# A decoder block on one core: the output projection as seven block products, its right operands built between the steps of the last attention-output products

## The chip, the core and the metric

The kernel runs on one core of one Trainium2 chip. The metric is the device time of one execution in microseconds (us). The core has engines that run side by side: TensorE (PE, matmuls into the accumulators of PSUM), VectorE (DVE), ScalarE (ACT), GpSimd (POOL) and SyncE (SP), whose queue issues nearly all DMA transfers of the part that is changed. Each engine takes its instructions in the order in which they were put into its queue, and waits on semaphores for the others.

## The reference, cut to what matters

One layer with SEQ = 2048 positions and D_MODEL = 1024 channels. Two branches (a gated recurrence and an attention in three window and dilation patterns) give `hr` and `o`; what the change touches is the end:

```python
y_rnn = (hr * silu(z_rnn)) @ w_out_rnn
y_attn = (o * silu(z_attn)) @ w_out_attn
merged = sigmoid(g_r + bg_r) * y_rnn + sigmoid(g_a + bg_a) * y_attn
x = x + gate[:, None, :] * (merged @ w_o)
return rms_norm(x, g_final)
```

## The kernel before, in words

All matmuls take float32 operands in two halves, a high and a low one, and do three matmuls (`mm3`, L149: high x high, high x low, low x high). The high half is a copy on ACT, the low half a subtraction on POOL (`lo_pool`) or DVE (`lo_dve`).

The input projection computes its large products by a scheme with seven block products in place of eight (`strassen`, L272). A left operand (two blocks of 128 columns, in two halves of the inner dimension) is turned into seven tiles `S` by sums on DVE (`left_operands`, L236), each split by `split_s`; the right operands B11, T2, T3, T1, B21, T4, B22 are held in SBUF. A product is 4 x 3 matmuls of 128x512; the products accumulate into four PSUM tiles X, Z, W, V, with three sums u1, u2, u3 on ACT and DVE between. In the first half of the sequence the `S` are built and also stored to memory, in the second they are loaded (`stored_operands`).

Then comes the attention, 16 heads of six units, laid out by hand in slots (`tc.manual_schedule`, L1381): in each slot run the scores of one unit, the softmax, the transposes and sums of earlier ones, and in between a number of steps of a generator, `steps` (L1277), the fill. It does the products with `w_out_rnn` (four jobs, one for each quarter n of the sequence) and with `w_out_attn` (two jobs, n = 0 and 1). A job has eight tiles m, a tile eight steps k, a step one `mm3`. Within a tile, SP gets in this order: a half tile of weights w at k = 1 (four buffers, so three halves ahead), the gates of the tile at k = 3 (`load_g`: gaT and mrT into two tiles of the ring "fg" of four buffers), the next half of w at k = 5, and at k = 7 the store of the tile before (meT). The eviction of the tile before stands at k = 1 on DVE. Near the end of a job the next job's left side y is loaded and split. `FILL` (L34) sets how many steps a slot gets: 3.6 in the first half of the heads, 3.2 in the second. Slots run from -5 to 105; the first rate holds for 60 of them, the second for 51. What is left of the fill runs behind the last slot.

After that the automatic scheduler takes over. Buffers for `w_o` are opened where the attention had its own; eight pieces of 128 rows of `w_o` are loaded, multiplied by the residual gate and split into `oh` and `ol` (L1429 to L1434). `output(n)` (L1436) does one quarter of the sequence: for each of four row blocks r it loads x and the merged columns from meT, splits these, does two halves of 512 columns of 8 x 3 matmuls, adds x, takes the mean square, scales, and stores. Between the four calls stand the attention-output products of n = 2 and 3 (`attn_product`, L1461), by `product` (L1254), which loads y, w and the gates in the scheduler's order with the same ring "fg" (`done_attn`, L1240).

Of the kernel before, what the change touches and what calls it, by code (L numbers as in the profile page):

```python
# [20 lines left out]
P = 128  # L21
S = 2048
# [11 lines left out]
FILL = (3.6, 3.2)  # L34
# [50 lines left out]
def decoder_block(ctx, tc, x, c, positions, g_norm, w_mod, b_mod, w_in, b_gate, conv_w, conv_b,  # L85
# [100 lines left out]
    def split_s(src):  # L186
        t = T(wq, [P, 2, KH, P], F32R, "S", bufs=7)
        last_hi[0] = nc.scalar.activation(t[:, 0], src, AF.Copy).ins  # L188
        lo_pool(t[:, 1], src, t[:, 0])
        return t  # L190
# [45 lines left out]
    def left_operands(pieces):  # L236

        a11, a12, a21, a22 = blocks(pieces)
        yield split_s(a11)
        s1 = T(wq, [P, KH, P], F32, "s1", bufs=1)  # L240
        s2 = T(wq, [P, KH, P], F32, "s2", bufs=1)
        nc.vector.tensor_tensor(s1[:], a21, a22, ALU.add)
        nc.vector.tensor_tensor(s2[:], s1[:], a11, ALU.subtract)
        yield split_s(s2[:])
        nc.vector.tensor_tensor(a21, a11, a21, ALU.subtract)
        yield split_s(a21)
        yield split_s(s1[:])
        yield split_s(a12)
        yield split_s(a22)
        nc.vector.tensor_tensor(s2[:], a12, s2[:], ALU.subtract)  # L250
        yield split_s(s2[:])

    def first_operands(x, pieces):

        for i, t in enumerate(left_operands(pieces)):
# [16 lines left out]
    def strassen(up, f, key, pieces, done):  # L272

        x = pair_id.setdefault(key, len(pair_id))
        ops = stored_operands(x) if f else first_operands(x, pieces)

        def prod(ps, b, first, last):
# [5 lines left out]
            n_prod[0] += 1  # L283
            run_late(n_prod[0])

        X = T(pj, [P, CH], F32, "pj")
        prod(X, "B11", True, False)
        Z = T(pj, [P, CH], F32, "pj")
# [6 lines left out]
        W = T(pj, [P, CH], F32, "pj")  # L295
# [4 lines left out]
        V = T(pj, [P, CH], F32, "pj")  # L300
# [933 lines left out]
    def done_rnn(ps, rows, cn):  # L1234
        g = T(fl, [P, CH], F32, "fg", bufs=4)
        nc.sync.dma_start(g[:], grT[rows, cn])
        nc.vector.tensor_tensor(g[:], ps[:], g[:], ALU.mult)
        nc.sync.dma_start(mrT[rows, cn], g[:])

    def done_attn(ps, rows, cn):  # L1240
        g = T(fl, [P, CH], F32, "fg", bufs=4)
        nc.sync.dma_start(g[:], gaT[rows, cn])
        r = T(fl, [P, CH], F32, "fg", bufs=4)
        nc.sync.dma_start(r[:], mrT[rows, cn])
        nc.vector.tensor_tensor(g[:], ps[:], g[:], ALU.mult)
        nc.vector.tensor_tensor(g[:], g[:], r[:], ALU.add)
        nc.sync.dma_start(meT[rows, cn], g[:])

# [4 lines left out]

    def product(w, ys, n, done):  # L1254

        cn = slice(n * CH, (n + 1) * CH)
        yt = []
        for k in range(KT):
# [7 lines left out]
        for m in range(KT):  # L1266
            rows = slice(m * P, (m + 1) * P)
            ps = T(pj, [P, CH], F32, "pj")
            for k in range(KT):
                if k % KH == 0:  # L1270
                    wt = load_wd(w, m, k // KH)
# [229 lines left out]
```

## Time and profile before

| What | us |
|---|---|
| median of 3 runs | 2367.67 |
| lowest and highest | 2366.49, 2369.38 |
| the profiled execution's own time | 2364.77 |
| its span in the profile | 2363.0 |

The profile is one execution. The page gives busy time, share of the span and instruction count of each engine, and then the span in 40 slices of 59 us with a digit for the busy tenths. PEld is the weight load, which overlaps PE. PEclk and "clock" are the granted clock of TensorE as a part of full speed. A timeline row has start, duration, engine, line, operation, output<-input, shape and count, and in brackets the idle time before it with the releaser. A row by windows has the stretch, its length, then busy time with the count for each engine, the clock, the mean busy share of the 16 DMA engines and GB/s. A row of the waits has who waited for whom, the total, the number of times and the longest. A row of a group has count, busy time, mean ns of one, and the idle time before it with its releasers. Lines L147, L161 and L164 are helpers. The tile names tell the groups apart: `pj` are projection products, `pq` the output projection, `fg` the gates, `w` the weights of the attention-output and recurrence-output products.

### The profile page before, as it was taken

To read this page: it belongs to the slowest core of one execution; us is meant where nothing else is said; L and a number is where in the kernel's file an instruction comes from. 1 tells how busy PE (TensorE), PEld (TensorE's weight loads), DVE (VectorE), ACT (ScalarE), POOL (GpSimd) and SP (SyncE) were. 2 spreads that over 40 slices of the span, in tenths; PEclk is the share of its full clock that TensorE was granted. 3 is DMA by queue.
4 is the path that set the end of the run, shared out by engine and by line. 5 is a ranking of instruction groups with operands and counts; after the bars stand their busy time and mean duration, and the time that the engine had idled before them with its cause. 6 is when DMAs were issued, how large, how long until landed. Compare 5 with 4: busy or idle time off the path is not lost.

```text
span 2363.0 us, 34030 instructions
## 1 busy us (share of the span) xinstructions
PE 2232.6 (94%) x11397; PEld 1877.8 (79%) x11397; DVE 1340.2 (57%) x2423; ACT 1170.4 (50%) x2332; POOL 1003.8 (42%) x765
## 2 busy tenths in 40 slices
PE   5999999999999989999999998799999999989998
PEld 5897777777777888888888877688888898978887
DVE  6847666666575653544444462266666777645433
ACT  3436656666642434655444410366667878622111
POOL 2566656665555553433121110355445656443000
PEclk9999999999999999999999999899999999999999
DMA  7266777777788639999776776888999889797652
GB/s 266 82 207 235 267 240 259 255 248 249 251 272 251 205 120 322 326 346 314 247 243 231 222 264 212 259 262 255 300 299 273 263 248 287 217 337 275 225 178 97
DMA packets 420902, 585.44 MB, mean 248 GB/s; under 512 B 72446, under 2 KB 278518, under 8 KB 419704
## 3 DMA queue, kind: packets, MB, share of 16 engines
q1 hardware_dynamic: 383288, 463.72, 62.9%
q10 hardware_dynamic: 37440, 119.55, 13.3%
q8 instruction: 90, 1.47, 0.2%
q14 instruction: 84, 0.69, 0.1%
HBM read 367.14 MB, written 216.01 MB: 247 GB/s over the span
## 4 chain that ended last, share of the span: by engine, by line
PE 61%; DMA 12%; DVE 11%; ACT 5%; issue 5%; POOL 3%; SPq 2%; ACTq 1%; DVEq 0%; POOLq 0%
PE pj L147 43%; PE pq L147 7%; PE o L147 3%; PE sc L147 3%; PE pg L147 2%; DMA wraw<-in_w_in_dram 2%; POOL S L161 1%; PE pT L1082 1%; DMA w<-wD 1%; DVE acc L487 1%; DMA wD<-s 1%; ACT S L188 1%; DMA kraw<-qT 1%; PE pT L1095 1%; DMA qT<-t 1%
## 5 line engine op out<-in xcount | busy, mean ns | idle before, releaser
L147 PE MATMUL pj<-T,S 128*128 128x512 f32 x4704 | 1119.5, 398 | 33.7 <-DVE ev L340 15.7
L147 PEld LDWEIGHTS pj<-T,S 128*128 128x128 f32 x4704 | 887.8, 189 | 254.0 <-DVE ev L340 21.1
L147 PE MATMUL pj<-yh,w 128*128 128x512 f32 x1024 | 371.7, 408 | 11.7 <-ACT yh L155 10.4
L161 POOL TENSOR_TENSOR S<-wraw,S 128x512 fp32r<-128x512 f32 x168 | 240.7, 1444 | 175.8 <-ACT S L188 100.5
L147 PEld LDWEIGHTS pj<-yh,w 128*128 128x128 f32 x1024 | 195.6, 191 | 50.3 <-ACT yh L155 12.5
L147 PE MATMUL pj<-yl,w 128*128 128x512 f32 x512 | 204.0, 399 | 2.3 <-POOL yl L161 1.4
L998 ACT ACTIVATE pp<-pp,st 128x256 f32<-128x256 f32 (+3 forms) x256 | 133.8, 524 | 89.5 <-DVE st L997 88.7
L147 PE MATMUL pj<-S,T 128*128 128x256 f32 x1152 | 161.9, 297 | 10.3 <-POOL S L161 7.0
L147 PEld LDWEIGHTS pj<-S,T 128*128 128x128 f32 x1152 | 151.9, 202 | 12.3 <-POOL S L161 8.0
L161 POOL TENSOR_TENSOR S<-s,S 128x512 fp32r<-128x512 f32 x84 | 114.7, 1366 | 89.7 <-ACT S L188 43.7
L164 DVE TENSOR_TENSOR ptl<-pT,pth 128x384 fp32r<-128x384 f32 (+1 forms) x160 | 97.8, 628 | 60.8 <-ACT pth L155 58.6
L1062 ACT ACTIVATE pp<-pp,M 128x256 f32<-128x256 f32 (+3 forms) x256 | 118.0, 523 | 12.7 <-DVE M L1186 12.7
L642 DVE SCALAR_TENSOR_TENSOR xc<-xr,par,xc 128x512 f32<-128x512 f32 x96 | 87.0, 907 | 61.2 <-ACT xc L636 58.1
L997 DVE CUSTOM_DVE_ANT_0 pp<-sc,msk 128x256 f32<-128x256 f32 (+3 forms) x256 | 105.2, 449 | 24.6 <-PE sc L147 21.4
L294 DVE TENSOR_TENSOR u<-pj,u 128x512 f32<-128x512 f32 x56 | 38.4, 686 | 140.8 <-PE pj L147 91.1
L147 PEld LDWEIGHTS pj<-yl,w 128*128 128x128 f32 x512 | 98.1, 192 | 18.5 <-POOL yl L161 2.6
L161 POOL TENSOR_TENSOR kq<-kraw,kq 128x512 fp32r<-128x512 f32 (+1 forms) x64 | 100.4, 1578 | 19.4 <-ACT kq L155 13.9
L161 POOL TENSOR_TENSOR vh<-vraw,vh 128x256 fp32r<-128x256 f32 (+1 forms) x64 | 66.4, 1037 | 94.8 <-ACT vh L155 83.1
L161 POOL TENSOR_TENSOR wh<-vraw,wh 128x640 fp32r<-128x640 f32 (+1 forms) x32 | 48.4, 1513 | 135.2 <-ACT wh L155 74.7
L147 PE MATMUL pq<-oh,mh 128*128 128x512 f32 x256 | 98.0, 394 | 7.9 <-ACT mh L155 7.9
L147 PE MATMUL pq<-ol,mh 128*128 128x512 f32 x256 | 100.8, 394 | 0.3 <-POOL ol L161 0.3
L147 PE MATMUL pq<-oh,ml 128*128 128x512 f32 x256 | 99.6, 390 | 0.0
(290 smaller groups left out, 3886.2 us busy)
## 6 DMA issues: line engine op xcount, KB each, us to landing
sD<-S ACTq DMA_DIRECT2D x196, 512.0 KB, 3.1
S<-sD SPq DMA_DIRECT2D x196, 512.0 KB, 5.4
w<-wD SPq DMA_DIRECT2D x128, 512.0 KB, 6.2
wraw<-in_w_in_dram SPq DMA_DIRECT2D x136, 256.0 KB, 3.3
wD<-s ACTq DMA_DIRECT2D x64, 256.0 KB, 4.1
T<-in_w_mod_dram SPq DMA_DIRECT2D x8, 1024.0 KB
vN<-ev SPq DMA_DIRECT2D x64, 128.0 KB, 2.5
zaT<-ev SPq DMA_DIRECT2D x32, 256.0 KB, 2.8
```

The lines of the kernel that those rows point to most:

```text
L147: last_mm[0] = nc.tensor.matmul(o, lhsT=l, rhs=r, start=st, stop=sp, **kw).ins
L161: nc.gpsimd.tensor_tensor(o, i, h.bitcast(F32), ALU.subtract)
L164: nc.vector.tensor_tensor(o, i, h.bitcast(F32), ALU.subtract)
L188: last_hi[0] = nc.scalar.activation(t[:, 0], src, AF.Copy).ins
L294: nc.vector.tensor_tensor(u2[:], Z[:], u1[:], ALU.add)
L487: nc.vector.scalar_tensor_tensor(acc[:], t[:, k, :], ca[:, k : k + 1], acc[:], ALU.mult, ALU.add)
L642: nc.vector.scalar_tensor_tensor(xc, xr[:, i : i + CH], cw(i), xc, ALU.mult, ALU.add)
L997: nc.vector.tensor_tensor_reduce(pdst, s_ps, mask, 1.0, 3e38, ALU.add, ALU.min, m_)
L998: nc.scalar.activation(pdst, pdst, AF.Exp, bias=m_, scale=-1.0, accum_out=l_)
L1062: nc.scalar.activation(pp, pp, AF.Copy, scale=w)
L1082: nc.tensor.transpose(pt[:, c0 + j * P : c0 + (j + 1) * P], pp[i][:, k * P : (k + 1) * P], ident)
L1095: nc.tensor.transpose(pt[:, c * P : (c + 1) * P], pp[:, half * P : (half + 1) * P], ident)
```

## The change

- The fill gets all eight jobs, with the attention-output products of n = 2 and 3 as its last two; `product`, `done_rnn`, `done_attn` and `attn_product` are gone. The second rate of `FILL` goes from 3.2 to 3.0. In the built program the order on SP within a tile stays: store, w, gaT, mrT, w.
- Behind the last slot the rest of the fill runs in the hand-written order, and at every second step one piece of `output_operands` is issued: loads of `w_o` (two row blocks at a time, two buffers), the gate multiplication, and the seven right operands by sums on DVE, split on ACT and on POOL or DVE. It has 54 pieces.
- `seven_products` is taken out of `strassen` as a function of its own. `output(n, r0)` uses it for two row blocks at a time: one load of the merged columns, seven left operands, 84 matmuls, and for each quarter of the result a sum on POOL (where the scheme has a u) and one on DVE. The normalisation writes in place.
- Buffers: the new left operands, x and u lie where w, y and fg were; the first pair's merged columns and its two first `S` buffers lie where the pieces of `w_o` were. PSUM has eight buffers for this part instead of four.

```diff
-FILL = (3.6, 3.2)
+FILL = (3.6, 3.0)
...
-    def split_s(src):
-        t = T(wq, [P, 2, KH, P], F32R, "S", bufs=7)
+    def split_s(src, new=lambda: T(wq, [P, 2, KH, P], F32R, "S", bufs=7)):
+        t = new()
...
-        ops = stored_operands(x) if f else first_operands(x, pieces)
-
+
+        def count():
+            n_prod[0] += 1
+            run_late(n_prod[0])
+
+        seven_products(stored_operands(x) if f else first_operands(x, pieces), B, pj, up, done, count)
+
+    def seven_products(ops, B, pp, up, done, count=lambda: None):
         def prod(ps, b, first, last):
...
+    def output_operands():
+        gate_b = T(ft, [P, D], F32, "gate_b")
+        nc.sync.dma_start(gate_b[:], gateD[0:1, :].broadcast_to([P, D]))
...
+        load(0)
+        load(1)
+        for _ in range(6):
+            yield
+        for k in range(KH):
+            t = raw.pop(k)
+            a1, a2, b1, b2 = (t[:, i, j * CH : (j + 1) * CH] for i in range(2) for j in range(2))
...
+            for i in range(2):
+                tt(t[:, i], t[:, i], gate_b[:], ALU.mult)
+                yield
+            split("B11", a1, lo_pool)
+            yield
+            split("B22", b2, lo_dve)
+            yield
+            split("B21", b1, lo_pool)
+            yield
+
+            tt(a1, a2, a1, ALU.subtract)
+            tt(a2, b2, a2, ALU.subtract)
+            yield
+            split("T1", a1, lo_pool)
+            tt(b2, b2, a1, ALU.subtract)
+            yield
+            split("T3", a2, lo_dve)
+            tt(b1, b1, b2, ALU.subtract)
+            yield
+            split("T2", b2, lo_pool)
+            yield
+            split("T4", b1, lo_dve)
+            yield
+            yield
+            if k + 2 < KH:
+                load(k + 2)
+            yield
...
-        fill = steps([(0, yaT, n) for n in range(NB)] + [(1, oT, n) for n in range(2)])
+        fill = steps([(0, yaT, n) for n in range(NB)] + [(1, oT, n) for n in range(NB)])
...
-        for _ in fill:
+        pools.close("ap", "sc", "pT", "po")
+
+        fp = pools.open("fp", bufs=1)
+        ft = pools.open("ft", bufs=1)
+        pieces = output_operands()
+        for i, _ in enumerate(fill):
+            if i % 2:
+                next(pieces, None)
+        for _ in pieces:
             pass
...
+    pools.close("ft", "fl", "wp", "pjb")
+    op = pools.open("op", side="right", bufs=1)
+    fo = pools.open("fo", bufs=1)
+    pq = pools.open("pq", bufs=8, space=PSUM)
...
+    def output(n, r0):
+
+        c0 = n * CH + r0 * P
+        i = NB // 2 * n + r0 // 2
+        raw = T(fo if i % 2 == 0 else op, [P, KT, 2 * P], F32, "mraw")
+        nc.sync.dma_start(raw[:], meT[:, c0 : c0 + 2 * P].rearrange("(k p) j -> p k j", p=P))
...
+        if i == 0:
+            new = lambda: T(fo, [P, 2, KH, P], F32R, "S", bufs=2)
+        else:
+            new = lambda: T(op, [P, 2, KH, P], F32R, "S", bufs=7)
...
+        def done(i, j, ps, u):
+            o = xo[i][:, j * CH : (j + 1) * CH]
+            if u is not None:
+                nc.gpsimd.tensor_tensor(o, o, u[:], ALU.add)
+            nc.vector.tensor_tensor(o, ps[:], o, ALU.add)
+            left[i] -= 1
+            if not left[i]:
+                t = xo[i]
...
+                nc.vector.scalar_tensor_tensor(t[:], t[:], ss[:, 1:2], gf[:], ALU.mult, ALU.mult)
+                nc.sync.dma_start(outv[n, r0 + i], t[:])
+
+        seven_products(left_operands(parts, op, lambda src: split_s(src, new)), WO, pq, op, done)
+
+    for n in range(NB):
+        for r0 in (0, 2):
+            output(n, r0)
```

145 lines of the change are left out of this document (44 added, 101 removed).

## The prediction

> **What bounds the kernel now.** First the page: the span, the engines' totals and the slices.
>
> ```profile
> span 2363.0 us, 34030 instructions
> PE 2232.6 (94%) x11397; PEld 1877.8 (79%) x11397; DVE 1340.2 (57%) x2423; ACT 1170.4 (50%) x2332; POOL 1003.8 (42%) x765
> PE   5999999999999989999999998799999999989998
> ```
>
> PE is busy 94% of the span, and the last slices, which the change touches, are at 8 or 9 tenths: what shortens PE's work there shortens the run, unless something else becomes late. Next, stages by windows (us, then PE, PEld, DVE, ACT, POOL busy with counts, clock, DMA share, GB/s): a stage that builds seven-product operands on the fly (300 to 700), one that loads them finished (1200 to 1360), the second half of attention (1880 to 1980), the gap behind attention, the stretch after it, and the mixed output and attention-output products (2160 to 2260).
>
> ```profile
> 300.00:700.00 400.00, 374.41 (x1582) 297.32 (x1581) 262.95 (x328) 238.62 (x392) 234.18 (x167) 0.99 0.75 256
> 1200.00:1360.00 160.00, 160.00 (x689) 129.10 (x688) 66.09 (x84) 75.83 (x115) 27.78 (x22) 1.00 0.75 236
> 1880.00:1980.00 100.00, 100.00 (x651) 90.53 (x651) 75.63 (x198) 79.79 (x190) 63.31 (x49) 1.00 0.86 261
> 2085.20:2092.90 7.70, 0.00 (x0) 0.00 (x0) 2.45 (x2) 3.03 (x3) 2.08 (x1) 0.81 1.09 355
> 2100.00:2135.00 35.00, 34.67 (x153) 28.37 (x152) 19.07 (x15) 6.89 (x7) 12.81 (x7) 1.00 1.05 380
> 2160.00:2260.00 100.00, 100.00 (x442) 82.85 (x441) 41.94 (x81) 17.59 (x31) 7.26 (x4) 1.00 0.71 234
> ```
>
> PE is full in attention and in the products behind it. Only at 2085 to 2093 does it stand, while the DMA engines are saturated (share above 1 at 355 to 380 GB/s until 2135). The timeline of PE gives that gap and the pitch of a 128x512 matmul:
>
> ```profile
> 2084.71 0.40 PE L147 MATMUL pj<-yh,w 128*128 128x512 f32 x1
> 2092.98 0.79 PE L147 MATMUL pq<-oh,mh 128*128 128x512 f32 x1 [7.87 <-ACT mh L155]
> 2093.57 0.63 PE L147 MATMUL pq<-ol,mh 128*128 128x512 f32 x1
> ...
> 2096.13 0.63 PE L147 MATMUL pq<-ol,mh 128*128 128x512 f32 x1
> ...
> 2199.93 0.39 PE L147 MATMUL pq<-oh,mh 128*128 128x512 f32 x1
> ...
> 2205.83 0.39 PE L147 MATMUL pq<-oh,ml 128*128 128x512 f32 x1
> ```
>
> 26 matmuls lie between the starts at 2199.93 and 2205.83: 0.227 us each. Between 2093.57 and 2096.13 lie six, 0.427 each: half rate after the gap.
>
> **Removed: 96 matmuls, and the gap.** Before, the output projection is 16 row blocks x 2 halves x 8 k x 3 = 768 matmuls; after, 8 pairs x 7 products x 4 k x 3 = 672. At 0.227 the old ones take 174.3 us. The new ones are like those of 1200 to 1360: 160 / 689 = 0.232 each, hence 156.0. Gain 18.3 us (21.8 if their pitch were 0.227). The gap goes too: before, the weights w_o are loaded, multiplied and split only when attention is over; after, this runs beside the attention-output products, and these run straight on. That frees 7.87 us, and 8 matmuls at 0.427 instead of 0.227, 1.6 us: 9.5. Together -27.8.
>
> **Moved: two thirds of the attention-output work into one block.** The fill gives 3.6 steps (three matmuls each) a slot over 60 slots, then 3.2, now 3.0, over 51: 379 steps are done when attention ends, now 369. Before, five steps and then the two 64-step products 2 and 3 followed, and the scheduler laid them among the output matmuls. After, 143 steps run alone: 143 x 3 x 0.227 = 97.4 us on PE, 5.45 us for a tile of eight steps. The ten steps that leave attention are a wash (0), as PE is full there (-2 to +3 for the job boundaries, which fall elsewhere).
>
> Alone, they ask much of the DMA. A tile moves two halves of w (512 KB each), gaT, mrT and its store (256 KB each): 1.84 MB; 17.9 tiles make 32.8 MB, the 16 loads of y 4.2, the eight of w_o with the gate 4.7: 41.7 MB. At 380 GB/s (the saturated window above) that is 109.7 us, 12 longer than PE needs.
>
> [...]
>
> But there is a tighter loop, in SP's queue. The ring of gate tiles "fg" has four buffers, two a tile, so the load of mrT for tile t+1 must wait until the store of tile t-1 has landed, and SP issues in order: the next half of w and the next store stand behind it. This queue in the product that runs nearly alone in the old kernel (2225 to 2270):
>
> ```profile
> 2248.78 0.32 SPq L1247 DMA_DIRECT2D meT<-fg  x1
> ...
> 2254.31 0.32 SPq L1244 DMA_DIRECT2D fg<-mrT  x1
> 2254.73 0.38 SPq L1251 DMA_DIRECT2D w<-wD  x1
> 2255.20 0.38 SPq L1247 DMA_DIRECT2D meT<-fg  x1
> ...
> 2260.97 0.32 SPq L1244 DMA_DIRECT2D fg<-mrT  x1
> ...
> 2261.86 0.38 SPq L1247 DMA_DIRECT2D meT<-fg  x1
> ```
>
> ```profile
> SPq L1244 <- DMA meT<-fg: 17.1, 6, 4.7
> ```
>
> ```profile
> w<-wD SPq DMA_DIRECT2D x12, 512.0 KB, 6.3
> meT<-fg SPq DMA_DIRECT2D x7, 256.0 KB, 5.5
> ```
>
> Six of the loads waited for a store, 17.1 us in all (the first row is total, times, longest; the other two end in KB and us to landing). From store to store it took 6.42 and 6.66 us, a mean of 6.54 against PE's 5.45. There it lasted a few tiles, and w, fetched up to two tiles ahead, covered it. The new block has 17 such tiles in a row with the same order in SP's queue (store, w, gaT, mrT behind the store, w, store). With two tiles of cover, 15 x 1.09 = 16.4 us come through to PE. On top, the gate and the first four w_o loads (2.62 MB) stand in SP's queue ahead of the next gaT, mrT and w: 2.62 / 0.380 = 6.9 us. The later w_o and y loads fit into the slack of the loop (1.84 MB / 6.54 us is 281 GB/s). Sum +23; the bounds are the bandwidth alone, +9 with two tiles prefetched, and, were a store 1.5 us slower under this load, 6.9 + 17 x 2.6 = +51, of which I keep +38, since a slower loop unloads the DMA. I take 23, as the loop is measured and its cover is small.
>
> **Added: operands by differences, and a new transition.** The rows that price them (ACT's high half, POOL's low half, DVE's sums):
>
> ```profile
> L188 ACT ACTIVATE S<-wraw 128x512 fp32r<-128x512 f32 x112 | 69.3, 623 | 30.8 <-PE pj L147 28.1 <-DMA wraw<-in_w_in_dram 1.4 <-DMA qT<-ev 0.8
> L161 POOL TENSOR_TENSOR S<-wraw,S 128x512 fp32r<-128x512 f32 x168 | 240.7, 1444 | 175.8 <-ACT S L188 100.5
> L243 DVE TENSOR_TENSOR s<-s,wraw 128x512 f32<-128x512 f32 x28 | 31.3, 1117 | 40.2 <-POOL S L161 40.0
> L242 DVE TENSOR_TENSOR s<-wraw,wraw 128x512 f32<-128x512 f32 x28 | 25.9, 926 | 51.3 <-DMA wraw<-in_w_in_dram 44.7 <-POOL S L161 6.5
> ```
>
> A pair of row blocks takes PE 84 x 0.232 = 19.5 us. POOL has seven low halves and three adds, 10 x 1.44 = 14.4; DVE four sums of about 1.1, six passes over PSUM of 0.69, and two normalisations, some 13; ACT some 8. All fit, and seven S buffers and eight PSUM banks let a pair run ahead. The built stage of the first half stood 25.6 of 400 us, mostly for an eviction:
>
> ```profile
> L147 PE MATMUL pj<-T,S 128*128 128x512 f32 x1500 | 358.6, 398 | 16.8 <-DVE ev L340 12.8 <-DVE zs L340 2.2 <-DVE u L299 1.7
> ```
>
> With five banks then and eight now I take +3 (0 to 10, the same 6.4% of 156). Building the right operands is hidden: 54 pieces at every second of the 143 steps are done by step 108 of it, some 35 steps before anything needs them; without that cover their POOL part alone, 16 x 1.44, would cost 23.
>
> First pair: its second product needs a sum on DVE that stands behind the last tile's eviction (some 1.7 us) and whose buffer lies where the last weights were: 1.7 + 0.93 + 1.12 + 0.62 + 1.44 = 5.8 us after the last product, while the first product covers 2.8. So PE stands 3.0 us. For the fifth, POOL's and ACT's queues have the next pair's first operand ahead, whose data come behind the last store, g_final and x (2.6 MB, 6.9 us, and SP's issues): about 1 us more. Stands of this size had a price once already (windows of 1 us: PE busy with its count, then the clock, DMA share, GB/s):
>
> ```profile
> 2002.00:2003.00 1.00, 0.00 (x0) 1.00 1.08 338
> 2005.00:2006.00 1.00, 1.00 (x5) 0.50 0.89 267
> ```
>
> PE stood from about 2001 to 2003 and then ran some four microseconds at half clock: +2. Transition +6 (3 to 9).
>
> The end: the last chain is as before (sum 0.69 to final multiply 1.28), but the other row's final multiply stands in front on DVE.
>
> ```profile
> 2354.58 0.69 DVE L1453 TENSOR_TENSOR xo<-pq,xo 128x512 f32<-128x512 f32 x1 [4.75 <-PE pq L147]
> ...
> 2357.98 1.28 DVE L1458 SCALAR_TENSOR_TENSOR ob<-xo,ss,gf 128x1024 f32<-128x1024 f32 x1
> ```
>
> +1 (0 to 1.3).
>
> Sum: -27.8 + 23 + 3 + 6 + 1 = +5. The profiled execution took 2364.8 (span 2363.0 and 1.8 around it), which gives 2370; the median of the runs is 2367.7, 2.9 above it, so 2373.
>
> **Rivals.** (B) The transfers keep up, and only the bandwidth counts: the loop is absorbed, because w runs two tiles ahead. Block +9, transition +4, products +1: -13.8, 2354. For it: PE was full at 380 GB/s from 2100 on; against it: that was a mix with output matmuls, which load far less. (C) The stands in the block bring the clock down tile by tile, as at 2005: four microseconds at half clock add 2 to PE's 5.45, so that PE itself needs 7.4 and the loop no longer hides it: 6.9 + 15 x 2 = 37, total +19, 2387. It decides once a stand in a tile reaches about 2 us; those expected are 1.1. [...] (D) Block and transition cost almost nothing (+3, +4, and 1 at the end): -20, 2348; it would take well over 400 GB/s. (E) The change doesn't bring its 18 us, since the built products stand as at 300 to 700, 10 instead of 3: 2380.
>
> **How the numbers follow.** The forecast 0.45, B 0.27, C 0.16, D 0.05, E 0.07. The forecast's own range is 2364 to 2384. The whole range, 2350 to 2389, takes in B and C and leaves out D and the outer ends. Within 0.2% (4.7 us, about what this kernel's measurement tells from none) lies a bit over a third of the forecast's case: 0.18. Faster: B, D and a few hundredths: 0.33. Slower: 0.49.
>
> **What would show it.** PE's matmuls fall by 96. The block behind attention takes 115 to 125 us instead of 97, SP's loads of mrT wait for meT's stores tile by tile, and PE waits for w. A stand of some 3 us comes before the second output product. The eight pairs take about 160 us. I am wrong if the block takes under 107 us (B), if its clock falls below 0.9 (C), or if the gain of the seven products is not there (E).

## The result and the profile after

| | before | after |
|---|---|---|
| median of 4 runs each, us | 2368.53 | 2391.39 |
| lowest and highest | 2366.49, 2370.42 | 2389.46, 2391.86 |
| ratio, with its 95% interval | | 1.0095 [1.0078, 1.0113] |
| span of the profiled execution | 2363.0 | 2389.6 |

The changed kernel is 0.95% slower, 22.9 us by the medians; the forecast was +5.3, and 2389 the end of its range. The page's totals and slices:

```profile
PE 2227.8 (93%) x11301; PEld 1861.7 (78%) x11301; DVE 1413.3 (59%) x2491; ACT 1199.2 (50%) x2400; POOL 1106.3 (46%) x845
...
PE   5899999999989899999999998899999999988997
```

PE has 96 matmuls fewer, as the change says, but POOL has 102 us more work and DVE 73, and the 36th and 37th slices, the block behind attention, are at 8 tenths. The two stretches behind the attention by windows (columns as before: length, then PE, PEld, DVE, ACT, POOL, the clock, DMA share, GB/s): first the block, from the last matmul of the attention's `o` to the first of the output projection, then the output part.

```profile
2070.90:2204.60 133.70, 113.74 (x449) 88.90 (x448) 64.06 (x81) 27.43 (x45) 36.00 (x26) 0.91 0.91 316
2204.60:2380.70 176.10, 162.60 (x673) 129.06 (x671) 125.28 (x182) 57.26 (x109) 112.18 (x79) 0.97 0.42 139
```

The block takes 133.7 us for 449 matmuls, which at 0.227 need 102. The output part takes 176.1 for 673, which at 0.231 (shown below) need 155.5. So 31.7 and 20.6 us are lost. PE's timeline tells where it stood (in brackets the stand and its releaser):

```profile
2093.20 0.76 PE L147 MATMUL pj<-yh,w 128*128 128x512 f32 x1 [7.90 <-DVE yl L164]
...
2103.37 0.50 PE L147 MATMUL pj<-yh,w 128*128 128x512 f32 x1 [2.14 <-DVE fg L1291]
...
2124.08 0.47 PE L147 MATMUL pj<-yh,w 128*128 128x512 f32 x1 [2.47 <-DMA w<-wD]
...
2144.39 0.47 PE L147 MATMUL pj<-yh,w 128*128 128x512 f32 x1 [2.09 <-DMA w<-wD]
...
2209.75 0.50 PE L147 MATMUL pj<-woT2h,S 128*128 128x512 f32 x1 [2.29 <-ACT S L188]
...
2220.52 0.79 PE L147 MATMUL pj<-woB11h,S 128*128 128x512 f32 x1 [2.87 <-ACT S L188]
...
2270.13 0.51 PE L147 MATMUL pj<-woT4h,S 128*128 128x512 f32 x1 [2.38 <-DVE u L304]
...
2292.36 0.79 PE L147 MATMUL pj<-woT4h,S 128*128 128x512 f32 x1 [2.44 <-DVE u L304]
...
2334.93 0.50 PE L147 MATMUL pj<-woT4h,S 128*128 128x512 f32 x1 [2.02 <-DVE u L304]
```

The stand of 7.87 us that the old kernel had at its transition is back, inside the block, with other stands of 2 us behind it; in the output part the first two pairs wait for a left operand, and later ones for `u3` ahead of the sixth product (T4). The first stand, from DVE's side, from the weight loads and from SP's queue:

```profile
2091.16 0.69 DVE L1291 TENSOR_TENSOR fg<-pj,fg 128x512 f32<-128x512 f32 x1 [9.23 <-DMA fg<-gaT]
...
2092.50 0.68 DVE L164 TENSOR_TENSOR yl<-yraw,yh 128x512 fp32r<-128x512 f32 x1
...
2093.17 0.29 PEld L147 LDWEIGHTS pj<-yh,w 128*128 128x128 f32 x1 [8.29 <-issue]
```

```profile
2075.28 1.35 SPq L1264 DMA_DIRECT2D yraw<-oT  x1
2076.72 0.59 SPq L1346 DMA_DIRECT2D gate_b<-gateD  x1
2078.16 2.89 SPq L1354 DMA_DIRECT2D wo<-in_w_o_dram  x4
2081.09 0.89 SPq L1286 DMA_DIRECT2D fg<-gaT  x1
...
2084.15 0.32 SPq L1241 DMA_DIRECT2D w<-wD  x1
```

The row of PE names a low half of y (L164, 2092.50) as the releaser, but that is the last thing to end before the start, not what PE needed: DVE makes the low halves of the odd steps, and the weight load of the first step had begun at 2093.17, before L164 ended at 2093.18. The semaphore updates in the trace show two things that came just before. The eviction of the tile before (L1291) waited 9.23 us for gaT and ended at 2091.85; gaT was issued at 2081.09, behind loads of y, the gate and four loads of `w_o`, and landed 10 us later. And the half of w for this tile, issued at 2084.15 behind the same loads, landed at 2093.07. So w came last, and the eviction ended 1.2 us before it. SP had at most eight transfers in flight there: none of its 116 later issues in the block starts before the eighth before it has landed, and this w went out 0.06 us after that. In e15_order (below), whose block differs in nothing up to there, the view names w itself:

```profile
2086.88 0.76 PE L147 MATMUL pj<-yh,w 128*128 128x512 f32 x1 [9.15 <-DMA w<-wD]
```

The DMA and the clock around the stand of the changed kernel (windows):

```profile
2085.00:2088.00 3.00, 0.31 (x2) 0.00 (x0) 0.00 (x0) 0.00 (x0) 0.00 (x0) 0.90 1.02 416
...
2093.00:2097.00 4.00, 3.80 (x9) 3.05 (x10) 0.19 (x1) 1.20 (x2) 1.28 (x1) 0.50 1.05 387
...
2104.00:2108.00 4.00, 4.00 (x12) 3.17 (x11) 3.97 (x5) 1.19 (x2) 1.97 (x2) 0.57 0.84 288
```

As the first stand begins, the DMA moves 416 GB/s over three microseconds, at a share of 1.02: it is full. PE runs at half clock behind it (0.50 from 2093 to 2097), and again from 2104, behind a stand of 2.14 us. Over windows of 1 us, busy time times what is missing of the clock gives 8.9 us in the block and 4.8 in the output part. Block: 102 + 20.0 of stands (133.70 - 113.74) + 8.9 = 131 of 133.7. The 2.8 that are left lie inside PE's busy time and were not followed further.

Where in the block the time goes can be counted from PE's timeline, by the end of every eighth step. Eight of the last seventeen tiles take 5.44 us, no more than PE needs. The excess is in the two behind the first job boundary (14.6 us), in the one behind the next pair of `w_o` rows (4.4, the stand at 2124.08), in the three around the second boundary, where two more rows of `w_o` meet the loads of y (11.3), and in the last four (2.2); together 32.5, as the borders differ a little.

DVE's work in the output part costs more than its rows of before said. The final multiplication and one of the small operations of the normalisation (count, busy, mean ns), before:

```profile
L1458 DVE SCALAR_TENSOR_TENSOR ob<-xo,ss,gf 128x1024 f32<-128x1024 f32 x16 | 21.6, 1347 | 0.6
...
L172 DVE TENSOR_TENSOR ss<-ss 128x1 f32<-128x1 f32 x16 | 2.7, 168 | 0.5
```

and after:

```profile
L1488 DVE SCALAR_TENSOR_TENSOR xo<-xo,ss,gf 128x1024 f32<-128x1024 f32 x16 | 30.5, 1908 | 0.4
...
L172 DVE TENSOR_TENSOR ss<-ss 128x1 f32<-128x1 f32 x16 | 7.9, 494 | 0.5
```

In the old kernel POOL was busy 28.8 us of the 263 behind 2100, and not at all behind 2186; now it is busy 112 of 176 us.

From span to span: the attention starts 4.2 us later, though the program up to there is the same (1516.5 against 1512.3; over the profiles below it starts between 1506 and 1517, so this is no effect of the change); it is 6.6 shorter, by its ten steps; everything behind it is 28.4 longer (309.8 against 281.3), and the end 0.5.

### The profile page after: what moved, and what is told of

Its sections match the earlier page's. It is cut to its first block, busy times and chain, and to the rows that moved or that the text cites. A ratio compares the mean times of both kernels' runs of the same rounds, so it can differ in the third digit from the quotient of the medians.

```text
span 2389.6 us, 34097 instructions
## 1 busy us (share of the span) xinstructions
PE 2227.8 (93%) x11301; PEld 1861.7 (78%) x11301; DVE 1413.3 (59%) x2491; ACT 1199.2 (50%) x2400; POOL 1106.3 (46%) x845
## 5 line engine op out<-in xcount | busy, mean ns | idle before, releaser
L161 POOL TENSOR_TENSOR S<-s,S 128x512 fp32r<-128x512 f32 x108 | 146.4, 1356 | 148.5 <-ACT S L188 112.7
L1003 ACT ACTIVATE pp<-pp,st 128x256 f32<-128x256 f32 (+3 forms) x256 | 133.7, 524 | 82.5 <-DVE st L1002 81.6
L164 DVE TENSOR_TENSOR ptl<-pT,pth 128x384 fp32r<-128x384 f32 (+1 forms) x160 | 97.8, 628 | 65.1 <-ACT pth L155 62.8
L299 DVE TENSOR_TENSOR u<-pj,u 128x512 f32<-128x512 f32 x64 | 43.8, 685 | 138.7 <-PE pj L147 84.5
L647 DVE SCALAR_TENSOR_TENSOR xc<-xr,par,xc 128x512 f32<-128x512 f32 x96 | 82.0, 854 | 66.2 <-ACT xc L641 63.0
L188 ACT ACTIVATE S<-s 128x512 fp32r<-128x512 f32 x108 | 67.4, 624 | 102.8 <-PE pj L147 43.4
L627 POOL TENSOR_TENSOR zs<-zs,sg 128x512 f32<-128x512 f32 x32 | 46.7, 1460 | 97.3 <-ACT sg L623 61.5
L188 ACT ACTIVATE S<-wraw 128x512 fp32r<-128x512 f32 x112 | 69.3, 622 | 32.5 <-PE pj L147 29.6
```

The source lines that it names most:

```text
L161: nc.gpsimd.tensor_tensor(o, i, h.bitcast(F32), ALU.subtract)
L164: nc.vector.tensor_tensor(o, i, h.bitcast(F32), ALU.subtract)
L299: nc.vector.tensor_tensor(u2[:], Z[:], u1[:], ALU.add)
L627: (2, lambda: nc.gpsimd.tensor_tensor(z[:], z[:], sg[0][:], ALU.mult))))
L647: nc.vector.scalar_tensor_tensor(xc, xr[:, i : i + CH], cw(i), xc, ALU.mult, ALU.add)
L1003: nc.scalar.activation(pdst, pdst, AF.Exp, bias=m_, scale=-1.0, accum_out=l_)
```

## The experiments

Two questions: what holds the block at +31.7, and what holds the output part at +20.6. Since the profiles differ by some microseconds ahead of the attention, the two stretches are read from the profile of each run, beside its time; the block is measured to the last step where the operands are built later. Six profiles whose block is the same in all but loads at its end have 133.7 to 138.4. The kernel before took 2368.5 us beside the changed kernel and 2360.6 to 2365.1 beside the experiments, so between rows the ratios are compared rather than the times.

| run | block | output part | us, median | ratio to before |
|---|---|---|---|---|
| changed kernel | 133.7 | 176.1 | 2391.4 | 1.0095 [1.0078, 1.0113] |
| e1_alone | 124.7 | 173.5 | 2429.3 | 1.0270 [1.0246, 1.0294] |
| e2_store | 135.3 | 174.9 | 2384.2 | 1.0076 [1.0047, 1.0105] |
| e3_actq | 134.1 | 175.7 | 2388.0 | 1.0099 [1.0072, 1.0126] |
| e4_early | 138.4 | 172.1 | 2391.3 | 1.0100 [1.0068, 1.0131] |
| e5_ring | 130.8 | 175.5 | 2387.8 | 1.0096 [1.0080, 1.0113] |
| e6_ring_alone | 114.4 | 172.0 | 2414.0 | 1.0218 [1.0196, 1.0241] |
| e7_norm | 135.6 | 170.3 | 2386.9 | 1.0093 [1.0078, 1.0109] |
| e8_ahead | 131.5 | 172.8 | 2384.3 | 1.0087 [1.0062, 1.0112] |
| e9_shift | 124.0 | 175.4 | 2376.0 | 1.0060 [1.0039, 1.0081] |
| e10_bank | 136.6 | 171.7 | 2385.0 | 1.0089 [1.0062, 1.0116] |
| e11_best | 126.8 | 169.0 | 2371.1 | 1.0045 [1.0031, 1.0058] |
| e12_swap | 136.6 | 165.0 | 2381.0 | 1.0078 [1.0061, 1.0095] |
| e13_spread | 122.3 | 174.7 | 2375.1 | 1.0050 [1.0034, 1.0066] |
| e14_all | 125.8 | 159.8 | 2363.1 | 1.0001 [0.9986, 1.0017] |
| e15_order | 135.7 | 162.3 | 2374.3 | 1.0059 [1.0038, 1.0079] |
| e16_fill | 115.3 | 162.9 | 2358.4 | 0.9985 [0.9975, 0.9994] |
| e17_pace | 120.5 | 160.0 | 2359.6 | 0.9995 [0.9982, 1.0008] |

**The block: loop, burst or order?** e1_alone builds the operands behind the fill.

```diff
-        for i, _ in enumerate(fill):
-            if i % 2:
-                next(pieces, None)
+        for _ in fill:
+            pass
         for _ in pieces:
             pass
```

> The pieces of the right operands (their loads of w_o and the gate too) are issued only behind the last step of the fill, so the attention-output steps behind the last slot run with no other work beside them. In the changed kernel that block took 133.7 us from the last matmul of the attention's o (2070.9) to the first output product (2204.6), where its 447 matmuls at 0.227 need 101.5. Theory A (the w_o traffic and the operand work in DVE's queue make the excess): the block falls to 104 to 110, and the clock stays 1.00 in it but for a job boundary. Theory B (the store loop of the gate ring, the forecast's term of 16.4): the loop is there without w_o too, so the block still takes 101.5 + 16 = 118 or more, with a stand of about 1 us in most tiles. In both the operands are now built in the open: four rounds of about 9.5 us on DVE (two gate products of 1.17, four sums and three low halves of about 1 each), 38 us; total about 2391 - 25 + 37 = 2403 by A, 2391 - 14 + 37 = 2414 by B.

The block fell by 9.0 only, to 124.7: theory A's 104 to 110 is out, and most of the excess is there without `w_o`. (The operands in the open cost 55 us, not 38.) What holds a tile there, by SP's loads of mrT and DVE's adds (L1293) in a stretch without y:

```profile
2107.08 0.32 SPq L1286 DMA_DIRECT2D fg<-mrT  x1
...
2113.45 0.32 SPq L1286 DMA_DIRECT2D fg<-mrT  x1
```

```profile
2106.36 0.69 DVE L1293 TENSOR_TENSOR fg<-fg,fg 128x512 f32<-128x512 f32 x1 [1.76 <-DMA fg<-mrT]
...
2112.74 0.69 DVE L1293 TENSOR_TENSOR fg<-fg,fg 128x512 f32<-128x512 f32 x1 [1.82 <-DMA fg<-mrT]
```

The load of mrT starts 0.02 us behind the end of the add (2112.74 + 0.69 = 2113.43), and that add waited for the load before it. One tile takes 6.37 us, where PE needs 5.45. So there is a loop of the length that I forecast (6.54), but through the add, since the pool hands the buffer that this add frees to the next mrT; the store isn't in it. PE waits for w behind it, some 0.6 us in such a tile. e2_store had tried the store:

```diff
-                if k == 7 and t:
+                if k == (4 if j > NB else 7) and t:
                     store(t - 1)
```

> The store of an evicted attention-output tile is issued three steps (2.0 us) earlier, at k = 4 instead of k = 7 (last three jobs), so that a store of 5.5 to 5.8 us lands before the load of mrT that needs its buffer is due, or nearly. Theory B (store loop): 17 tiles lose most of their 1.1 us, SP's waits for meT's stores fall from 22.0 us to under 6, block -12 to -16, total 2375 to 2379. Theory A: SP's waits shorten too, but PE waits elsewhere (a DVE queue blocked by a late gate at the job boundaries, w behind w_o), so the time falls by 0 to 4, to 2387 to 2391.

The block stayed at 135.3, and SP's waits for meT's stores rose from 22.0 us to 31.9. The edit moved waits and took none away, so alone it decides little. e3_actq gave the loads of `w_o` and the gate to ACT's queue:

```diff
-                nc.sync.dma_start(t[:, i], w_o[0, (k + i * KH) * P : (k + i * KH + 1) * P, :])
+                nc.scalar.dma_start(t[:, i], w_o[0, (k + i * KH) * P : (k + i * KH + 1) * P, :])
```

> Only the queue of the w_o and gate loads changes: ACT's instead of SP's, at the same steps. Theory A1 (head of the line in SP's queue: gaT, mrT and w are issued behind the burst): gaT at the first job boundary lands some 5 us earlier, the stand of 7.9 us at 2093 falls below 4, and with the half clock after it and the stands behind the later w_o pairs the time falls by 8 to 12, to 2379 to 2383. Theory A2 (the burst shares the same 16 DMA engines whichever queue it is in): gaT lands as late, the time stays within 3 of 2391. Theory B: within 7 (its 6.9 for the burst), the stand per tile stays.

The stand of 7.9 became two, 2.5 and 4.4 (the second for w), and the block stayed at 134.1: A2's time, though gaT came earlier, as A1 said (the eviction ends 17 us behind the attention instead of 21). The edit does not decide between queue and volume: ACT's queue now held the high halves of y behind these loads,

```profile
2082.02 2.19 ACT L155 ACTIVATE yh<-yraw 128x512 fp32r<-128x512 f32 x4 [18.90 <-DMA fg<-gaT]
```

and the same bytes were issued at the same steps, so volume is not ruled out. Then the ring (L1286): mrT in two buffers of its own behind the attention, with the operands beside (e5_ring) and behind the fill (e6_ring_alone).

```diff
-                g = T(fl, [P, CH], F32, "fg", bufs=4)
+                g = T(fx[0], [P, CH], F32, "fm", bufs=2) if src is mrT and fx else T(fl, [P, CH], F32, "fg", bufs=4)
```

> Behind the attention the loads of mrT get two buffers of their own, and the four of the ring serve gaT and the stores. In the run with the operands built later the load of mrT for the next tile started 0.04 us behind the add of the tile before, which itself waited for mrT's landing: it was given the buffer that this add frees, so one tile took 6.34 us (landing 5.6, add 0.69). Theory L (this loop, through the add and not through the store, holds the block): the waits of SP behind mrT and the add go, block from 133.7 to 120-126, total 8 to 14 below 2391, 2377 to 2383. Rival W (the weights w are late anyway, behind y and w_o and in a queue that has eight transfers in flight): PE's waits for w and for the job boundary stay, total within 4 of 2391.

> Both edits: mrT in buffers of its own, and the operands built behind the fill. With the operands behind, but the old ring, the attention-output block took 124.7 us (its 149 steps need 102). Theory L: only the job boundaries are left, block 106 to 112, and total 2429 less 13 to 19, 2410 to 2416. Rival W: the stands for w stay, block 119 or more, total 2423 or more.

With both edits the block is 114.4, 2.4 above L's range, the ratio falls by 0.0052 (12 us, L's 13 to 19 just missed), and the halves of w are fetched at PE's pace:

```profile
2094.14 0.32 SPq L1242 DMA_DIRECT2D w<-wD  x1
...
2099.58 0.32 SPq L1242 DMA_DIRECT2D w<-wD  x1
```

5.44 us from one to the next (every second half is shown), the 24 matmuls of a tile. The loop is broken, and rival W's 119 is out. The 2x2: old ring 133.7 and 124.7, own buffers 130.8 and 114.4. With `w_o` out of the way the loop is worth 10.3; with it there only 2.9, which the spread between profiles covers, since the burst then sets the pace. So e5_ring by itself went as rival W said, and only e6_ring_alone shows the loop.

What is left there, 12.4 us, lies at the two job boundaries: by tile 3.6 us at the first and 9.1 at the second, and all tiles between them take 5.44. First boundary, second, and the stretch between them:

```profile
2076.70:2087.60 10.90, 9.12 (x34) 5.73 (x34) 3.81 (x7) 2.53 (x4) 2.56 (x2) 1.00 1.03 396
2118.40:2137.00 18.60, 13.62 (x50) 8.78 (x50) 5.43 (x9) 5.05 (x8) 5.12 (x4) 1.00 0.96 350
2087.00:2118.00 31.00, 31.00 (x139) 25.64 (x138) 7.61 (x11) 0.00 (x0) 0.00 (x0) 1.00 0.95 328
```

At the first the DMA is full (396 GB/s, share 1.03). At the second it moves 350 GB/s, and PE waits for w and then for the high halves of y; the loads of y have four buffers, so the later four start only when an earlier split has freed one. No run changed the loads of y, so volume and this short lead are not told apart there. e8_ahead issued the gates a tile earlier, on top of e5_ring:

```diff
+                if k == 4 and fx and t + 1 < len(tiles):
+                    load_g(t + 1)
```

> As with mrT in buffers of its own, and gaT and mrT are issued nearly a tile earlier behind the attention (at k = 4 of the tile before), so that an eviction doesn't wait for them and DVE goes on to the low halves of y. Theory A (DVE's queue, blocked by an eviction that waits for gates, makes the boundary's stand of 7.9 us): that stand falls to under 3 and with its half clock 6 to 8 us go beyond the ring alone, total 2369 to 2376. Rival W (the burst of w_o, the gate, y and now the gates too delays w itself): the stand stays above 5 and PE's releaser there is w; total within 3 of the ring alone.

The stand was 9.7 us and its releaser w, as rival W said, but theory A was not tried by it: DVE's queue was as blocked as before, since the gates of the boundary's tile were still issued behind the burst.

```profile
2085.29 0.69 DVE L1292 TENSOR_TENSOR fg<-pj,fg 128x512 f32<-128x512 f32 x1 [9.58 <-DMA fg<-gaT]
```

The low halves of y followed at once, and w still came 1.3 us after them. e9_shift starts the pieces behind the job boundary (on top of e5_ring), and e13_spread also loads the rows of `w_o` one pair at a time:

```diff
-            if i % 2:
+            if i >= 18 and i % 3 < 2:
                 next(pieces, None)
```

> With mrT in buffers of its own, the pieces of the right operands start 18 steps behind the last slot instead of at once, just past the first job boundary (step 15), and come at two of three steps, so that all but the last loads of w_o lie between the two boundaries. The 2x2 of before: block 133.7 (old ring, operands beside), 130.8 (own buffers, beside), 124.7 (old ring, behind), 114.4 (own buffers, behind). Theory T (what costs is w_o's burst falling together with the eight loads of y and the boundary's DVE work): the stand of 8.3 us at the first boundary goes below 2, and the block falls to 118 to 124, total 2377 to 2383 (ring alone 2388). Theory V (the volume: 41.7 MB through eight transfers in flight need what they need, wherever they start): the stands move to the middle of the block, block 127 or more, total 2384 or more.

> As with mrT's own buffers and the pieces past the first boundary (block 124.0), with the pairs of w_o rows loaded one at a time, 12 pieces (12 us) apart, instead of two at once. Theory T (bursts): the stand of 4.9 us behind the first loads of w_o falls below 1.5, with the half clock behind it 5 to 6 us go, block 118 to 120, total 2369 to 2372. Rival V (volume): the stand moves to the second boundary, where a pair now lands beside y: block within 2 of 124, total 2374 to 2378.

With the shift alone the block fell to 124.0 (theory T's 118 to 124, just), the boundary's stand to 1.0; a new one of 4.9 for w came behind the first `w_o` loads. Spread, that one halved, but another came at the second boundary:

```profile
2098.43 0.47 PE L147 MATMUL pj<-yh,w 128*128 128x512 f32 x1 [2.36 <-DMA w<-wD]
...
2138.85 0.47 PE L147 MATMUL pj<-yh,w 128*128 128x512 f32 x1 [3.78 <-DVE wo L1386]
```

(Here too the named releaser is a coincidence: L1386 is a sum for an operand, which ended as the matmul began. By the semaphores PE waited for w, issued at 2130.17 behind two rows of `w_o` and landed at 2138.71; the eviction had ended at 2137.30. The stand of 4.1 us in e14_all is the same.) The block is in rival V's range, the ratio 0.001 below e9_shift's.

**The output part: why is u3 late?** e4_early issues the second pair's columns ahead of g_final and x:

```diff
+        if i == 0:
+            raws[1] = load_me(1, 2 * P)
```

> The merged columns of the second pair of row blocks are loaded right behind those of the first, ahead of g_final and the first x. If the stand of 2.87 us at 2220.5 and the half clock behind it (some 3.4 us, 1.7 lost) come from the late landing of these columns (10.4 us after an issue at 2209.5), both go: -4 to -5, total 2386 to 2387. Rival: DVE is late there anyway or the two loads delay each other, and the stand moves to the first pair: within 2 of 2391. In the block nothing changes by either theory.

The stand of 2.87 went and the output part fell by 4.0, as expected; the total didn't show it, as the block of that profile was 4.7 longer. e7_norm shares the small operations of the normalisation between the two rows of a pair (128x2 instead of two times 128x1), and e10_bank (without that) gives the sixth product of the output part a PSUM tile of its own:

```diff
-        prod(W, "T4", False, True)
-        done(1, 0, W, u2)
+            W = T(pp, [P, CH], F32, "pj")
+            prod(W, "T4", True, True)
+            done(1, 0, W, u3)
```

> On top of the early load of the second pair's columns (output part 172.1 us instead of 176.1, alone): the normalisation of the two rows of a pair shares its chain of small operations, seven on DVE and one on ACT for two rows instead of for one. In the changed kernel these small operations on DVE took 28 us over seven pairs (the multiplications of 128x1 with 0.54 to 0.78 us each), 4 a pair. Theory N (the sixth product stands since u3 comes late out of a full DVE queue): 2 us a pair are freed, the waits before the products of T4 fall from 8.9 us to under 4, output part 164 to 168, total 2379 to 2384. Rival P (the order is what counts: u3 stands behind the long final multiplications of 2.0 us whatever precedes them): waits within 2 of 8.9, output part 171 to 173, total 2386 to 2389.

> On top of the early load of the second pair's columns: the sixth product goes into a PSUM tile of its own instead of being added on to the third's, and the quarter takes u3 (which holds the third's) where it took u2. So the sixth product no longer waits for DVE's reading of the third. Theory N (that wait, 8.9 us in the sum, and the half clock behind it): no stand before T4's products, output part from 172.1 to 161-164, total 2380 to 2383. Rival P (DVE is full, so that the next thing that PE needs from it, the sums for the left operands or the reading of V ahead of the seventh product, is late instead): new stands of the same sum before other products, output part 169 or more, total 2387 or more.

e7_norm gained 1.8 only: rival P, mostly. In e10_bank PE's wait moved, from u3 to the reading of V ahead of the seventh product. PE's waits in the output part, e4_early, then e10_bank (total, times, longest):

```profile
PE pj L147 <- DVE u L304: 9.1, 5, 4.4
```

```profile
PE pj L147 <- DVE xo L1492: 6.7, 5, 4.1
```

So DVE is late as a whole, not with u3. DVE's timeline in e7_norm shows with what:

```profile
2260.39 1.26 DVE L1498 TENSOR_TENSOR ss<-ss 128x2 f32<-128x2 f32 x1
2261.69 1.22 DVE L1499 TENSOR_SCALAR ss<-ss 128x2 f32<-128x2 f32 x1
2262.94 1.21 DVE L1500 TENSOR_TENSOR ss<-ss 128x2 f32<-128x2 f32 x1
2264.19 3.47 DVE L1503 SCALAR_TENSOR_TENSOR xo<-xo,ss,gf 128x1024 f32<-128x1024 f32 x2
...
2268.19 0.68 DVE L304 TENSOR_TENSOR u<-pj,u 128x512 f32<-128x512 f32 x1
```

Three operations on two numbers a partition take 1.2 us each, where such a one took 0.17 in the old output part (L172 above) and the one just before them in this run 0.16 (L1497, at 2260.19). In the changed kernel such operations took up to 1.3 beside one of POOL's and 0.16 without (last section). Then come two final multiplications, and only then u3 (L304). e12_swap turns the order of DVE and POOL round (on top of e7_norm), and e15_order also issues the normalisation behind the next pair's reading of V:

```diff
-                nc.gpsimd.tensor_tensor(o, o, u[:], ALU.add)
-            nc.vector.tensor_tensor(o, ps[:], o, ALU.add)
+                nc.vector.tensor_tensor(t[:], ps[:], u[:], ALU.add)
+                nc.gpsimd.tensor_tensor(o, o, t[:], ALU.add)
```

> On top of the early columns and the shared normalisation chain (output part 170.3 us, waits for u3 7.1): DVE first adds PSUM and u into a tile, and POOL adds that to x afterwards, where before DVE stood for POOL's x + u ahead of reading PSUM (9.7 us of DVE's waits in seven pairs). Theory D (DVE in order behind POOL is what makes u3 and the reading of V late): waits for u3 below 4, output part 164 to 167, total 2380 to 2384. Rival P2 (what is late is the chain of the normalisation and its long multiplications of 1.8 us, each slowed by POOL, that stand ahead of u3): waits within 2 of 7.1, output part 169 to 171, total 2385 to 2388.

> As with the order of DVE and POOL changed round, and the normalisation of a pair issued on DVE only behind the next pair's u3 and its reading of V, so that nothing of it stands ahead of what PE waits for. Theory P2: the waits for u3 and for V go, output part 159 to 163 (156 plus the first stand and what is left), total 2376 to 2381. Theory D: no more than 2 beyond the run before it. Rival F (DVE and POOL are simply full): the stands come before the left operands instead, output part 167 or more.

165.0 and 162.3. Both orders count: D is worth 5.3 us, P2 another 2.7. u3 was waited for once in each (3.0 and 1.5 us), F is out. Some of it goes back at the end: from the last product to the end of the span it is 8.9 us in the changed kernel, 9.7 in e7_norm and 11.1 from e12_swap on.

**All together.** e11_best joined own buffers, the shift, the early columns, the shared chain and the PSUM tile; e14_all the spread and the two orders instead of that tile.

> All together: mrT's own buffers, the pieces past the first boundary, the early columns, the shared normalisation chain and the sixth product in a tile of its own. By theories T and N the parts add up: block 118 to 124, output part 159 to 164, so 2391 less 10 to 16 less 12 to 17, 2358 to 2369, against 2365 to 2368 for the kernel before: level with it or slightly faster. By V and P: 2380 or more.

> All together: mrT's own buffers, spread pieces past the first boundary, early columns, the normalisation behind V's reading, DVE ahead of POOL. By theories T and P2: block 118 to 120, output part 159 to 163, so about 2391 - 15 - 15 = 2361, against 2361 to 2368 for the kernel before: 0.990 to 1.001 of it. By V and F: 2370 or more, slower than before.

e11_best still lost 0.45%: its PSUM tile only moved the stand. e14_all is level with the kernel before, though both blocks (126.8 and 125.8) lie above theory T's ranges. Its output part, a full stretch and the whole:

```profile
2271.00:2341.00 70.00, 70.00 (x303) 56.77 (x302) 49.40 (x64) 25.31 (x46) 46.55 (x35) 1.00 0.42 151
2191.90:2351.70 159.80, 156.96 (x673) 125.99 (x671) 108.92 (x137) 54.65 (x100) 106.44 (x78) 1.00 0.43 150
```

70 us with 303 matmuls, 0.231 each, at full clock: the seven products have the price that was forecast, once DVE is in time. e17_pace then moved the `w_o` loads clear of both boundaries, and e16_fill besides put the ten steps back:

```diff
-FILL = (3.6, 3.0)
+FILL = (3.6, 3.2)
```

> As with all edits together (block 125.8, output part 159.8), with the rate of the fill back at 3.2 (ten steps more in the attention, ten fewer behind it, so the first job boundary and most of its loads of y come under the attention) and the pieces of the operands placed so that each pair of w_o rows is loaded clear of the y loads and some 15 us before DVE multiplies it. Forecast's term (the ten steps are a wash, -2 to +3): the block falls by 10 x 0.684 = 6.8 and the attention grows as much; with the stands at 2099 (3.7) and 2141 (4.1) and their half clock gone by the placing, total 2351 to 2356, against 2363 for the kernel before on the same chip. Theory T (a step costs more behind the attention, 0.84 us with its stands, than in it, 0.68, as the DMA has room there): 2 to 5 us more are gained than e17_pace shows. Rival V (volume): the stands stay some 8 us and the total is within 3 of 2362.

> The same placing with the rate of the changed kernel (3.0). If the stand of 4.1 us (DVE's gate multiplication waits for its w_o rows, and the eviction stands behind it) is a matter of when the rows are loaded, it goes, with its half clock some 6 us of the block's 125.8; the block is 117 to 120 and the total 2355 to 2358. Rival V: the stands move, block 123 or more, total 2361 or more.

e17_pace has a block of 120.5, half a microsecond over its range, a time 1.6 over its own, and is level with the kernel before; the 4.1 us stand is gone, as w no longer stands behind `w_o` there. e16_fill's block is 115.3 for 139 steps (95 us), 1.9 of it the first output product's wait for its operand, so its excess is that of e17_pace (18.5). It gains 1.2 on e17_pace by the medians, 1.6 by the means with some 3 either way, and the pieces start a few steps earlier in it too: a wash, which doesn't exclude theory T's 2 to 5. It is faster than the kernel before, by 0.15% [0.06%, 0.25%], and short of its expected time. What still stands in its block is y and w:

```profile
2079.76 0.50 PE L147 MATMUL pj<-yh,w 128*128 128x512 f32 x1 [3.79 <-ACT yh L155]
...
2120.79 0.47 PE L147 MATMUL pj<-yh,w 128*128 128x512 f32 x1 [1.85 <-DMA w<-wD]
```

The DMA isn't out of it, and the rest wasn't tried.

## Why the forecast was wrong

**Removed, -27.8.** Right: 96 matmuls, at 0.231 where 0.232 was taken. The old stand is gone from its place.

**Ten steps out of attention, a wash.** Right: attention fell by 6.6, e16_fill against e17_pace gave 1.2, within the noise.

**The block, +23; it was +31.7.** The terms were 16.4 for the loop, 6.9 for the burst and nothing for the rest. Three steps failed. The first is the loop's price, 15 tiles of 1.09 coming through to PE: in the changed kernel the tiles away from the loads take 5.44, and own buffers for mrT gave 2.9 only (e5_ring). The loop is real, and its length was right, but it costs its 10.3 (e1 less e6) only where `w_o` is out of the way; its cause was right in part, as I read the store's landing as what releases the buffer, and SP did wait 22.0 us for stores, but in the stretch of e1_alone that shows the loop it was the add. The second is the burst, right in mechanism (w behind `w_o` in SP's queue; the stand is 7.9) and too small: with the half clock and the stand behind it the first boundary cost 14.6 instead of 6.9. The third is "the later w_o and y loads fit into the slack of the loop", put at nothing: they cost 15.7 (4.4 and 11.3), as I compared averages. At a boundary eight loads of y, 2.1 MB, come on top of two tiles' 3.7 MB within 11 us, and that is 530 GB/s, where the full DMA moved 416 (row 2085). Even without `w_o` and the ring 12.4 are left (114.4 - 102), all of it at the boundaries. So the sum came within 9 us by luck: a term that was hardly there stood in for two that were left out or small. That PE waits for w came true, though tile by tile only where no burst lay on top. That the clock would cost 8.9 I had only in rival C. It was right in the mechanism and wrong in the place: the stands are at the bursts, the clock over the block 0.91.

**Transition, +6.** 5.2 us of stands (2.29 and 2.87) and a half clock behind each, some 8.4 in all. The first was named rightly; the second came not at the fifth product but at the next pair, from the same cause (its columns behind the last store, g_final and x), and e4_early took it away.

**Inner stalls, +3 (0 to 10).** The step that failed is "all fit". Taking 5.2 of stands and two of the three stretches at half clock (3.2 of 4.8) for the transition, some 12 of the 20.6 are left, 8.1 of them in four waits for u3 and 1.6 in the half clock behind one. I counted some 13 us of DVE a pair; it was 125.3 / 8 = 15.7 busy, with DVE standing behind POOL's sums besides. My 13 left some 2.2 for a row's normalisation, the final multiplication at 1.28 us and the small operations at 1, their prices with POOL idle; they took 1.91 and 1.9. e7, e12 and e15 together gave back 9.8 (172.1 to 162.3). E came true in substance, by DVE's order instead of the eviction of PSUM.

**The end, +1.** 0.5.

Of +17.6 by which the medians missed the forecast, 8.7 are the block and 11.6 the output part (20.6 for 9); the removed side brought some 3 more than forecast.

## What to carry to other kernels

Work that is hidden by an average may not be hidden in the window where it runs: sum the transfers over each job boundary, and place bursts between them. When an engine's queue serves what PE waits for, put its PSUM reads ahead of everything that waits for another engine, and of long work that nobody waits for. And price an operation from a stretch where the other engines are as busy as they will be: here DVE's work beside POOL cost 1.4 to 3 times its rows of before.

## What the runs showed of the hardware

- DVE beside POOL: in the changed kernel's output part the final multiplication took 2.28 us in the ten of sixteen cases that ran beside an operation of POOL and 1.28 in the six that did not, a 128x1 product (L172, L175) up to 1.3 and 0.16, the sums for the left operands up to 1.8 and 0.69. Reads of PSUM with one SBUF input stayed at 0.68 either way (L304). No such operation was longer without POOL beside it, and each stretched one ended a fixed time behind POOL's: 0.02 us for the small, 0.55 for the sums, 1.08 for the final multiplications. All this waiting is 43 of DVE's 125 us.

```profile
2327.72 1.29 POOL L161 TENSOR_TENSOR S<-s,S 128x512 fp32r<-128x512 f32 x1 [3.94 <-ACT S L188]
2327.82 1.21 DVE L172 TENSOR_TENSOR ss<-ss 128x1 f32<-128x1 f32 x1
```

  All the stretched ones of the changed kernel read two operands from SBUF. The 128x2 `TENSOR_SCALAR` of 1.22 us (e7_norm) reads one tile only, while those of 128x1 in the changed kernel stayed at 0.14 to 0.22 beside POOL; no run shows why.
- The clock: a stand of 2.14 us in the block was followed, 1.1 us after PE ran again, by 3.4 us at half clock, while the stands of 1.20 and 1.52 in e14_all's output part cost nothing (clock 1.00). Three of five stands of 2.0 to 2.9 us in the changed kernel's output part were followed by half clock, the ones at 2270.13 and 2334.93 were not. In the profiles of the kernel before and of the changed one the 31 and 41 changes of the clock all lie whole multiples of 3.41 us apart, and what goes with them is how long PE stood between two such points: of the 541 windows of 3.41 us at full clock behind 1400 us, all 16 with 1.90 us or more of stands were followed by half clock, none of the 515 with less than 1.3, and two of the ten between. In the changed kernel the stand of 2.29 lay in one window, that of 2.38 was cut by a point and left 1.80 in the longer part:

```profile
2206.89:2210.30 3.41, 1.12 (x5) 0.45 (x3) 2.59 (x4) 1.81 (x3) 0.53 (x1) 1.00 0.69 147
2210.30:2213.71 3.41, 3.41 (x9) 2.62 (x9) 1.75 (x1) 0.00 (x0) 1.99 (x2) 0.50 0.88 222
2268.33:2271.74 3.41, 1.61 (x7) 1.34 (x8) 2.82 (x3) 0.00 (x0) 3.41 (x3) 1.00 0.55 222
2271.74:2275.15 3.41, 3.41 (x17) 2.75 (x16) 2.82 (x3) 0.63 (x1) 3.41 (x4) 1.00 0.50 148
```
